# Three products of 256 columns in place of 512 + 256 for the first token half, and weight sums and low parts of the feed-forward stage on GpSimd

## The chip, the cores and the metric

The kernel runs on one core of a Trainium2 chip. The metric is the device time of one execution in microseconds (us), median of several. The core has a matrix engine (TensorE, PE in the profile, its weight loads PEld), three engines for elementwise work (VectorE or DVE, ScalarE or ACT, GpSimd or POOL) and SyncE (SP), whose queue issues the loads here. Matmuls write to PSUM, in banks of 512 float32 columns; weights and activations lie in SBUF.

## The reference, cut to what matters

One layer of an encoder step for two groups of requests that share the weights: 512 prompt tokens and 64 sample tokens, 576 in all, with 1024 features.

```python
xn = _rmsnorm(x, p['ln_mix'])
proj = xn @ p['w_in']
conv_in, z, a, b, qd, kd, vd = jnp.split(proj, SPLIT_AT, axis=-1)
...
oa, S_new = _gdn_chunked(qa, ka, va, g, beta, S0.astype(jnp.float32))
...
ob = _diff_attention(qd.reshape(B, L, H_DIFF, 2, D_DIFF), k_all.reshape(B, Lk, H_DIFF, 2, D_DIFF),
                     v_all, q_pos, k_pos, lam)
...
h = x + jnp.concatenate([oa, ob], axis=-1) @ p['w_out']
h = h + _mem_attn(_rmsnorm(h, p['ln_mem_q']), mem_k, mem_v, p['w_mem_q'], p['w_mem_o'])
hn = _rmsnorm(h, p['ln_ffn'])
h = h + jnp.square(jax.nn.relu(hn @ p['w_ff1'])) @ p['w_ff2']
```

w_ff1 is 1024 x 4096, w_ff2 4096 x 1024; a final norm gives y. Everything is float32.

## The kernel before, in words

**Products in three parts.** Activations are kept transposed, features on the 128 partitions and tokens along the columns. Each operand of a large product is split in two float32r numbers: the high part is a rounding copy (ScalarE), the low part the rest (VectorE, source minus high part). A product is then high x high + high x low + low x high, all summed in one PSUM bank.

**Token halves.** HALVES cuts the 576 tokens into columns 0 to 255 and 256 to 575 (256 and 320 columns). project (line 167) computes one block of 128 output features: for each half it takes a bank "pr" (three of them in turn) and loops over the 128-row slices k of the weights, 8 for a weight of 1024 rows and 4 (kt=4) for a group of the second feed-forward layer. For the second half, high_parts (line 183) issues two matmuls of 320 columns with the high weights, on the tokens' high part and on their low part, and project a third with the low weights. For the first half the two with the high weights are one matmul: its moving operand is both parts side by side, 512 columns, and the bank's two halves take high x high (with low x high added there) and high x low. Every matmul has a weight load of its own.

**The way out of a bank.** project calls evac with the bank and, for the first half, with the bank's other half as "more". add_to (line 191) copies "more" to the target on ScalarE and adds the bank to it on VectorE. The evacs are: conv_input (inputs of the short convolution), project_z, diff_project's evac (q, k, v of the attention heads), add_residual (adds to the residual stream hT, a second time for "more"), split_query, add_group (sums of the second feed-forward layer, likewise a second add) and last_block. The a/b columns (around line 496) go the same way by hand.

**Order of work.** A framework for tiles puts in the semaphores, gives out buffers (a tile waits until the previous owner of its buffer has been read), and sets the order on each engine by priorities (tc.high_priority, tc.issue_after). Each engine then runs its queue in order. First come the norm and the input projection with the convolution; then the chunked scan and the attention heads, with projections between them; the memory keys and values, the output projection, the memory attention; then the feed-forward stage.

**The feed-forward stage** (from about 545 us). The first layer is cut into 16 pairs of 128-column blocks. Each pair (ff1_pair, line 1466) is one step of a two-by-two scheme with seven products instead of eight: split_pair (line 1393) takes the raw quarters A11, A21, A12 and A22 of the pair's weights and forms A21 + A22 (line 1402), A11 - A21 (1407), s1 - A11 (1408) and A12 - A11 (1415), in place but for the first, each 128 x 512 on VectorE; halves_to (lines 1356 and 1357) splits quarters and sums into high (ScalarE) and low parts (VectorE). The products run in the order 1, 5, 6, 2, 7, 3, 4, each 12 matmuls of 288 columns. keep (line 1494) copies an intermediate sum out of a bank on ScalarE, and put applies the squared ReLU and splits the result. The pair's weights lie in tiles "wh", "wl" (two buffers each) and "w4" (three), the raw ones in "raw" (three).

Between pairs run blocks of the second layer, four to a pair: weights2 (line 1462) loads 512 rows of a 128-column block into "r2", split (lines 1455 to 1459) makes "w2h" on ScalarE and "w2l" on VectorE (three buffers each), and project runs with kt=4. split_first forms the first pair's parts on VectorE, and last_weights those of the last group.

Of the kernel before, what the change touches and what calls it, by code (L numbers as in the profile page):

```python
# [15 lines left out]
P = 128  # L16
D = 1024
KT = 8
# [19 lines left out]
def hybrid_layer_kernel(  # L38
# [127 lines left out]

    def project(w, x, evac, kt=KT, halves=HALVES, between=None):


        for a0, n in halves:  # L170
            b = bank("pr")
            for k in range(kt):
                low_part = lambda: mm(b[:, :n], w[1][:, k, :], x[k // 4][:, 0, k % 4, a0 : a0 + n], start=False, stop=False)
                if k == kt - 1:
                    low_part()
                high_parts(b, w[0], x, k, a0, n, kt)
                if k < kt - 1:
                    low_part()
            if between and a0 == 0:
                between()  # L180
            evac(b[:, :n], a0, n, None if a0 else b[:, 256:])

    def high_parts(b, w, x, k, a0, n, kt=KT):
        xk = x[k // 4][:, :, k % 4, a0 : a0 + n]
        if a0 == 0:
            mm(b.rearrange("p (j n) -> p j n", j=2), w[:, k, :], xk, start=k == 0, stop=k == kt - 1)
        else:
            mm(b[:, :n], w[:, k, :], xk[:, 0], start=k == 0, stop=False)
            mm(b[:, :n], w[:, k, :], xk[:, 1], start=False, stop=k == kt - 1)

    def add_to(dst, b, more):
        A.copy(dst, more)
        V.tensor_tensor(dst, b, dst, ALU.add)

# [115 lines left out]
    def conv_input(m, tag="cb"):  # L310
        cbs[m] = cb = small(tag, [P, 584])
        G.memset(cb[:, 0:3], 0.0)

        def evac(b, a0, n, more):
            if a0 == 0 and more is None:
                A.copy(cb[:, 3:259], b)
            elif a0 == 0:
                add_to(cb[:, 3:259], b, more)
            else:
                A.copy(cb[:, 3 + a0 : 259 + a0], b[:, :256])  # L320
                A.copy(cb[:, SOFF + 3 : SOFF + 3 + DEC], b[:, 256:])

        return evac
# [24 lines left out]
    def second(m):  # L348

        a0, n = HALVES[1]  # L350
        b = bank("pr")
        for pw, px in (HH, LH, HL):
            for k in range(KT):
                mm(
                    b[:, :n], wts[m][pw][:, k, :], xs[k // 4][:, px, k % 4, a0 : a0 + n],
                    start=(pw, px) == HH and k == 0, stop=(pw, px) == HL and k == KT - 1,
                )
        ev[m](b[:, :n], a0, n, None)

# [3 lines left out]
    with in_order() as opened:  # L363
# [38 lines left out]
        ev = {4: conv_input(4)}  # L402
        ev[4](fb[4][:, :256], 0, 256, None)
        first(5, HL, LH)
# [11 lines left out]
        ev[5] = conv_input(5)  # L416
        ev[5](fb[5][:, :256], 0, 256, None)
        for q in range(2):
# [3 lines left out]
        ev[6] = conv_input(6, "an")  # L422
        ev[6](fb[6][:, :256], 0, 256, None)
        second(4)
# [71 lines left out]
    for a0, n in HALVES:  # L496
        b = bank("pr")
        for k in range(KT):
            high_parts(b, wab2, xs, k, a0, n)
        if a0:  # L500
            V.tensor_copy(abT[:, a0 : a0 + n], b[:16, :n])
        else:
            add_to(abT[:, :n], b[:16, :256], b[:16, 256:])
    V.tensor_copy(abT[:, T:], abT[:, SEQ:T])
# [132 lines left out]
    def project_z():  # L637
        for h in range(H):
            def evac(b, a0, n, more):
                z = zs[:, h, a0 : a0 + 256]  # L640
                with tc.high_priority():
                    if more is not None:
                        add_to(z, b, more)
                        b = z
                    A.activation(z, b[:, :256], AF.Silu)
                    if a0:
                        A.activation(zsample[:, h, :], b[:, 256:], AF.Silu)

            project(weights(w2, 1536 + h * P), xs, evac)
# [315 lines left out]
    def diff_project(h):  # L965
# [8 lines left out]
        for kind, base in (("q", 2056), ("k", 2568), ("v", 3080)):  # L974
            def evac(b, a0, n, more):
                ts_ = slice(a0, a0 + n)
# [7 lines left out]
                if kind == "q":  # L984
                    d = b
                    if more is not None:
                        d = qn[1][:, ts_].bitcast(F32)
                    with tc.high_priority():
                        if more is not None:
                            add_to(d, b, more)  # L990
                        parts(qn, d)
                    if a0:
                        for c in range(2):
                            R = slice(64 * c, 64 * c + 64)
                            A.copy(qz[R, R], d[R, n - DEC :])
                            for j in range(2):
                                nc.sync.dma_start(
                                    qs[h % 2][64 * j : 64 * j + 64, c, :SEQ].bitcast(F32), qn[j][R].bitcast(F32)
                                )
                    return  # L1000
                d = small("zr", [P, 320])[:, :n] if kind == "v" else kdT[:, h, ts_]
                with tc.high_priority():
                    if more is not None:
                        add_to(d, b, more)
                    else:
                        V.tensor_copy(d, b)
                if kind == "k":
# [206 lines left out]
    def add_residual(m, last, split=None, g0=None, alone=None):  # L1214


        def evac(b, a0, n, more):
            hm = hT[m // 4][:, m % 4, a0 : a0 + n]
            V.tensor_tensor(hm, hm, b, ALU.add)
            if more is not None:  # L1220
                V.tensor_tensor(hm, hm, more, ALU.add)
            if not last:
                return
            if split is not None:
                split_to(split, hm, m, a0, gcol[:, g0 + m : g0 + m + 1])
            if m == 0:
                if a0 == 0:
                    accs[0] = const([P, T], "accq")
                A.activation(accs[0][:, a0 : a0 + n], hm, AF.Square)
            else:  # L1230
                sq = temps(n)
                A.activation(sq, hm, AF.Square)
                if alone is not None:
# [44 lines left out]
    for h in range(H):  # L1278
        qh = [small("kd" if h % 2 else "aT", [P, T], dt=F32R) for i in range(2)]
        ql = cp.tile([P, 2, T], F32R, tag=f"qz{h % 2}", name=nm("ql"))  # L1280
        for i in range(2):
            def split_query(b, a0, n, more):
                if more is not None:
                    q = small("zr", [P, 320])[:, :n]
                    add_to(q, b, more)
                    b = q
                A.copy(qh[i][:, a0 : a0 + n], b)
                V.tensor_tensor(ql[:, i, a0 : a0 + n], b, qh[i][:, a0 : a0 + n].bitcast(F32), ALU.subtract)

            project(weights(w_mem_q[0], (2 * h + i) * P), hx, split_query)  # L1290
# [103 lines left out]
    def split_pair(p):  # L1394
# [6 lines left out]
        with tc.high_priority() if p > 1 else ExitStack():  # L1401
            V.tensor_tensor(s1, A21, b[:, :, P:], ALU.add)
            ws[1] = low_and_high(wtile("wh", wide_))
            halves_to(*ws[1], A11)
            ws[5] = low_and_high(wtile("wh", wide_))
            halves_to(*ws[5], s1)
            V.tensor_tensor(A21, A11, A21, ALU.subtract)
            V.tensor_tensor(A11, s1, A11, ALU.subtract)
            t = [wtile("wl", raw_) for _ in range(2)]
# [4 lines left out]
            ws[2], ws[4] = ([x[:, :, c : c + P] for x in t] for c in (0, P))  # L1414
            V.tensor_tensor(A12, A12, A11, ALU.subtract)
            ws[3] = low_and_high(ft("w4", wide_, 3, F32R))
# [36 lines left out]
    def split(src, tag, bufs, urgent):  # L1453
        shape = list(src.shape)
        wh, wl = (ft(tag + x, shape, bufs, F32R) for x in "hl")
        with tc.high_priority() if urgent else tc.issue_after(put_last[1]):
            A.copy(wh, src)  # L1457
            V.tensor_tensor(wl, src, wh.bitcast(F32), ALU.subtract)  # L1458
        return wh, wl
# [75 lines left out]
    def add_group(g, m):  # L1535
        def evac(b, a0, n, more):
            am = (accu[0] if g < SCALED else hT)[m // 4][:, m % 4, a0 : a0 + n]
            if g == 0:
                if more is not None:
                    add_to(am, b, more)  # L1540
                else:
                    A.copy(am, b)  # L1542
                return
            V.tensor_tensor(am, am, b, ALU.add)  # L1544
            if more is not None:
                V.tensor_tensor(am, am, more, ALU.add)  # L1546

        return evac
# [21 lines left out]
    def last_block(m, s, a0, n, alone=None):  # L1570
        hi, lo = (view(u, m // 4, 16, P)[:, 4 * (m % 4) : 4 * (m % 4) + 4] for u in wlast)

        def evac(b, a0, n, more):
            add_residual(m, True, alone=alone)(b, a0, n, more)
            hm = hT[m // 4][:, m % 4, a0 : a0 + n]
# [141 lines left out]
```

## Time and profile before

| | |
|---|---|
| median of 3 runs | 976.82 us (976.27 to 977.54) |
| span of the profiled execution, first to last instruction | 975.3 us |
| granted TensorE clock, mean | 0.998 |
| feed-forward stage, 550 to 950 us: VectorE busy | 300.95 us |
| the same: ScalarE busy | 215.13 us |
| the same: GpSimd busy | 0.00 us |
| bytes read from memory | 79.93 MB, 92 GB/s over the span with the writes |

The profile is of one execution, and its times are to be compared with its own span; the span leaves out 1.5 us of the median time. In rows of groups stand the line, engine, operation, output and inputs, shapes and count, then the busy time (us) and the mean duration (ns), then idle time before them and who ended it. In rows of the timeline stand start and length in us; matmuls overlap, so their lengths say less than the distance from one start to the next. A release "<-ACT keep L1494" is worked out from semaphores.

### The profile page before, as it was taken

The page shows a single profiled execution, that of the slowest core. Times are in us where ns is not written, and L with a number is a line of the kernel's source. Part 1 is how long each engine was busy: PE and PEld are TensorE (multiplying, and loading weights), DVE is VectorE, ACT ScalarE, POOL GpSimd, SP SyncE. Part 2 cuts the span into 40 slices and gives each one's busy share as a digit, 9 for nine tenths or more (in the row PEclk, how much of TensorE's full clock was granted, in tenths as well). Part 3 has the DMA queues.
Part 4 walks back from the last instruction along what each step waited for, and adds up shares of the span by engine and source line. Part 5 has one row for each costly group of instructions (what it writes and reads, how often), then busy time and mean ns, then how long its engine had stood idle before and what let it go on. Part 6 is the DMA issues. An engine that isn't in the chain of part 4 may idle for free.

```text
span 975.3 us, 16991 instructions
## 1 busy us (share of the span) xinstructions
PE 960.4 (98%) x6399; PEld 889.9 (91%) x6399; DVE 689.4 (71%) x1508; ACT 536.9 (55%) x1218; POOL 66.6 (7%) x158
## 2 busy tenths in 40 slices
PE   9999999998999999999999999999999999999996
PEld 7999998997888878999999999999999999999996
DVE  6655777776867776666657888567867779978674
ACT  6664774533656765435445567665544444545444
POOL 4341020211010000000000000000000000000000
PEclk9999999999999999999999999999999999999999
DMA  7442332120744666341121423332323223322202
GB/s 209 117 138 77 95 125 66 46 64 23 187 122 122 219 182 196 87 130 44 45 65 44 141 69 96 90 88 88 87 81 87 87 87 87 87 87 87 66 23 97
DMA packets 124915, 96.01 MB, mean 98 GB/s; under 512 B 6204, under 2 KB 112846, under 8 KB 124322
## 3 DMA queue, kind: packets, MB, share of 16 engines
q1 hardware_dynamic: 124466, 94.28, 33.6%
q8 instruction: 50, 0.82, 0.4%
q10 hardware_dynamic: 368, 0.66, 0.2%
q14 instruction: 31, 0.25, 0.1%
HBM read 79.93 MB, written 9.75 MB: 92 GB/s over the span
## 4 chain that ended last, share of the span: by engine, by line
PE 58%; issue 2%; DVE 1%; ACT 1%; DMA 0%; POOLq 0%; POOL 0%; ACTq 0%; DVEq 0%; SPq 0%
PE pr L107 37%; PE ba L107 10%; PE g L107 6%; PE gs L107 4%; PE ba L113 1%; DMA raw<-in_w_ff_dram 0%; ACT u L1596 0%; ACT c L1504 0%; DVE u L1552 0%; DVE w2l L1458 0%; ACT c L1503 0%; DVE w L1357 0%; DVE wl L1357 0%; DVE wh L1357 0%; ACT wl L1356 0%
## 5 line engine op out<-in xcount | busy, mean ns | idle before, releaser
L107 PE MATMUL pr<-u,wh 128*128 128x320 f32 (+2 forms) x1240 | 325.9, 341 | 0.1
L107 PE MATMUL pr<-u,wl 128*128 128x256 f32 (+1 forms) x816 | 226.1, 301 | 0.0
L107 PEld LDWEIGHTS pr<-u,wh 128*128 128x128 f32 x1240 | 212.1, 189 | 15.2 <-ACT u L286 0.3
L107 PEld LDWEIGHTS pr<-u,wl 128*128 128x128 f32 x816 | 150.5, 189 | 2.5 <-DVE wl L387 0.2
L160 DVE TENSOR_TENSOR wl<-raw,wh 128x1024 fp32r<-128x1024 f32 x65 | 79.5, 1223 | 56.5 <-ACT wh L159 56.3
L159 ACT CAST wh<-raw 128x1024 fp32r<-128x1024 f32 x65 | 68.2, 1049 | 61.9 <-PE pr L107 46.6
L107 PE MATMUL pr<-u,w2h 128*128 128x320 f32 (+1 forms) x384 | 98.5, 341 | 0.0
L1457 ACT CAST w2h<-r 128x512 fp32r<-128x512 f32 x56 | 34.7, 620 | 87.6 <-PE pr L107 85.4
L107 PE MATMUL pr<-f,w2h 128*128 128x320 f32 (+1 forms) x288 | 74.5, 341 | 0.5 <-DVE u L1546 0.5
L107 PEld LDWEIGHTS pr<-u,w2h 128*128 128x128 f32 x384 | 65.0, 188 | 4.5 <-ACT u L1542 0.3
L107 PE MATMUL pr<-u,w2l 128*128 128x256 f32 (+1 forms) x256 | 65.2, 296 | 0.0
L1544 DVE TENSOR_TENSOR u<-u,pr 128x256 f32<-128x256 f32 x96 | 42.4, 450 | 17.1 <-PE pr L107 16.5
L206 POOL TENSOR_TENSOR tiny<-tiny,nhalf 128x1 f32<-128x1 f32 (+4 forms) x10 | 8.8, 879 | 651.3 <-DVE tiny L1610 514.1
L107 PE MATMUL ba<-u,wl 128*128 128x288 f32 x360 | 52.9, 296 | 0.0
L107 PEld LDWEIGHTS pr<-f,w2h 128*128 128x128 f32 x288 | 48.8, 188 | 4.5 <-issue 1.7
L107 PEld LDWEIGHTS ba<-u,wl 128*128 128x128 f32 x360 | 49.2, 188 | 0.6 <-ACT keep L1494 0.5
L107 PE MATMUL pr<-f,w2l 128*128 128x256 f32 (+1 forms) x192 | 48.9, 295 | 0.0
L107 PEld LDWEIGHTS pr<-u,w2l 128*128 128x128 f32 x256 | 47.0, 189 | 1.5
L1458 DVE TENSOR_TENSOR w2l<-r,w2h 128x512 fp32r<-128x512 f32 x56 | 38.5, 688 | 9.6 <-ACT w2h L1457 9.4
L107 PE MATMUL pr<-wh,u 128*128 128x512 f32 x128 | 41.6, 400 | 0.1
L1503 ACT ACTIVATE c<-c 128x288 f32<-128x288 f32 x48 | 20.6, 443 | 28.5 <-DVE c L1502 28.5
L107 PEld LDWEIGHTS pr<-f,w2l 128*128 128x128 f32 x192 | 35.2, 189 | 1.1
(552 smaller groups left out, 2024.8 us busy)
## 6 DMA issues: line engine op xcount, KB each, us to landing
raw<-in_w_ff_dram SPq DMA_DIRECT2D x36, 512.0 KB
raw<-in_w_in_dram SPq DMA_DIRECT2D x28, 512.0 KB
r<-in_w_ff_dram SPq DMA_DIRECT2D x56, 256.0 KB
raw<-in_w_mem_k_dram SPq DMA_DIRECT2D x8, 512.0 KB
raw<-in_w_mem_v_dram SPq DMA_DIRECT2D x8, 512.0 KB
raw<-in_w_out_dram SPq DMA_DIRECT2D x8, 512.0 KB
raw<-in_w_mem_q_dram SPq DMA_DIRECT2D x8, 512.0 KB
raw<-in_w_mem_o_dram SPq DMA_DIRECT2D x8, 512.0 KB
```

Source lines behind the costliest of these rows:

```text
L107: i = nc.tensor.matmul(out, lhsT, rhs, start=start, stop=stop, skip_group_check=skip_group_check)
L113: i = nc.tensor.transpose(out, in_, ident[:n, :n])
L159: A.copy(wh, raw)
L160: V.tensor_tensor(wl, raw, wh.bitcast(F32), ALU.subtract)
L206: G.tensor_tensor(out, in_, bc(nhalf[: in_.shape[0], 0:1], list(in_.shape)), ALU.pow)
L1457: A.copy(wh, src)
L1458: V.tensor_tensor(wl, src, wh.bitcast(F32), ALU.subtract)
L1503: A.activation(c, c, AF.Relu)
L1544: V.tensor_tensor(am, am, b, ALU.add)
```

## The change

Two things are changed.

First, project runs the three products of both halves alike, as three matmuls of the half's own columns into the same columns of the bank. So evacs get no "more", and add_to and high_parts go; evacs read the bank directly. The a/b columns follow.

Second, in the feed-forward stage the four sums of split_pair and the low part in split (second layer's weights) are issued on GpSimd (G) in place of VectorE (V). halves_to, split_first and last_weights stay as they are.

```diff
-    def project(w, x, evac, kt=KT, halves=HALVES, between=None):
+    def project(w, x, evac, kt=KT, halves=HALVES):
         for a0, n in halves:
             b = bank("pr")
             for k in range(kt):
-                low_part = lambda: mm(b[:, :n], w[1][:, k, :], x[k // 4][:, 0, k % 4, a0 : a0 + n], start=False, stop=False)
-                if k == kt - 1:
-                    low_part()
-                high_parts(b, w[0], x, k, a0, n, kt)
-                if k < kt - 1:
-                    low_part()
-            if between and a0 == 0:
-                between()
-            evac(b[:, :n], a0, n, None if a0 else b[:, 256:])
+                xk = x[k // 4][:, :, k % 4, a0 : a0 + n]
+                passes = [(0, 0), (0, 1), (1, 0)] if k < kt - 1 else [(1, 0), (0, 0), (0, 1)]
+                for j, (jw, jx) in enumerate(passes):
+                    mm(
+                        b[:, :n], w[jw][:, k, :], xk[:, jx],
+                        start=k == 0 and (jw, jx) == (0, 0), stop=k == kt - 1 and j == 2,
+                    )
+            evac(b[:, :n], a0, n)
...
-    def high_parts(b, w, x, k, a0, n, kt=KT):
-        xk = x[k // 4][:, :, k % 4, a0 : a0 + n]
-        if a0 == 0:
-            mm(b.rearrange("p (j n) -> p j n", j=2), w[:, k, :], xk, start=k == 0, stop=k == kt - 1)
-        else:
-            mm(b[:, :n], w[:, k, :], xk[:, 0], start=k == 0, stop=False)
-            mm(b[:, :n], w[:, k, :], xk[:, 1], start=False, stop=k == kt - 1)
-
-    def add_to(dst, b, more):
-        A.copy(dst, more)
-        V.tensor_tensor(dst, b, dst, ALU.add)
...
                 with tc.high_priority():
-                    if more is not None:
-                        add_to(z, b, more)
-                        b = z
                     A.activation(z, b[:, :256], AF.Silu)
...
                 with tc.high_priority():
-                    if more is not None:
-                        add_to(d, b, more)
-                    else:
-                        V.tensor_copy(d, b)
+                    V.tensor_copy(d, b)
...
             V.tensor_tensor(hm, hm, b, ALU.add)
-            if more is not None:
-                V.tensor_tensor(hm, hm, more, ALU.add)
...
         with tc.high_priority() if p > 1 else ExitStack():
-            V.tensor_tensor(s1, A21, b[:, :, P:], ALU.add)
+            G.tensor_tensor(s1, A21, b[:, :, P:], ALU.add)
...
-            V.tensor_tensor(A21, A11, A21, ALU.subtract)
-            V.tensor_tensor(A11, s1, A11, ALU.subtract)
+            G.tensor_tensor(A21, A11, A21, ALU.subtract)
+            G.tensor_tensor(A11, s1, A11, ALU.subtract)
...
-            V.tensor_tensor(A12, A12, A11, ALU.subtract)
+            G.tensor_tensor(A12, A12, A11, ALU.subtract)
...
             A.copy(wh, src)
-            V.tensor_tensor(wl, src, wh.bitcast(F32), ALU.subtract)
+            G.tensor_tensor(wl, src, wh.bitcast(F32), ALU.subtract)
...
             V.tensor_tensor(am, am, b, ALU.add)
-            if more is not None:
-                V.tensor_tensor(am, am, more, ALU.add)
```

conv_input, diff_project's q, split_query and add_group's first group change in the same way as z and k/v: the call of add_to goes, and the copy, cast or difference that followed reads the bank.

More of the change, by code (lines that the diff above doesn't have):

```diff
@@ L312, in conv_input, with evac @@
         G.memset(cb[:, 0:3], 0.0)
-        def evac(b, a0, n, more):
-            if a0 == 0 and more is None:
+        def evac(b, a0, n):
+            if a0 == 0:
                 A.copy(cb[:, 3:259], b)
-            elif a0 == 0:
-                add_to(cb[:, 3:259], b, more)
             else:
@@ L357, in second @@
                 )
-        ev[m](b[:, :n], a0, n, None)
+        ev[m](b[:, :n], a0, n)
     def turn_half(t, q):
@@ L402, in hybrid_layer_kernel @@
         ev = {4: conv_input(4)}
-        ev[4](fb[4][:, :256], 0, 256, None)
+        ev[4](fb[4][:, :256], 0, 256)
         first(5, HL, LH)
@@ L416, in hybrid_layer_kernel @@
         ev[5] = conv_input(5)
-        ev[5](fb[5][:, :256], 0, 256, None)
+        ev[5](fb[5][:, :256], 0, 256)
         for q in range(2):
@@ L422, in hybrid_layer_kernel @@
         ev[6] = conv_input(6, "an")
-        ev[6](fb[6][:, :256], 0, 256, None)
+        ev[6](fb[6][:, :256], 0, 256)
         second(4)
@@ L498, in hybrid_layer_kernel @@
         for k in range(KT):
-            high_parts(b, wab2, xs, k, a0, n)
-        if a0:
-            V.tensor_copy(abT[:, a0 : a0 + n], b[:16, :n])
-        else:
-            add_to(abT[:, :n], b[:16, :256], b[:16, 256:])
+            for j in range(2):
+                mm(b[:, :n], wab2[:, k, :], xs[k // 4][:, j, k % 4, a0 : a0 + n], start=k == j == 0, stop=k == KT - 1 and j == 1)
+        V.tensor_copy(abT[:, a0 : a0 + n], b[:16, :n])
     V.tensor_copy(abT[:, T:], abT[:, SEQ:T])
@@ L638, in project_z, with evac @@
         for h in range(H):
-            def evac(b, a0, n, more):
+            def evac(b, a0, n):
                 z = zs[:, h, a0 : a0 + 256]
                 with tc.high_priority():
-                    if more is not None:
-                        add_to(z, b, more)
-                        b = z
                     A.activation(z, b[:, :256], AF.Silu)
@@ L974, in diff_project, with evac @@
         for kind, base in (("q", 2056), ("k", 2568), ("v", 3080)):
-            def evac(b, a0, n, more):
+            def evac(b, a0, n):
                 ts_ = slice(a0, a0 + n)
@@ L984, in evac @@
                 if kind == "q":
-                    d = b
-                    if more is not None:
-                        d = qn[1][:, ts_].bitcast(F32)
                     with tc.high_priority():
-                        if more is not None:
-                            add_to(d, b, more)
-                        parts(qn, d)
+                        parts(qn, b)
                     if a0:
@@ L994, in evac @@
                             R = slice(64 * c, 64 * c + 64)
-                            A.copy(qz[R, R], d[R, n - DEC :])
+                            A.copy(qz[R, R], b[R, n - DEC :])
                             for j in range(2):
@@ L1002, in evac @@
                 with tc.high_priority():
-                    if more is not None:
-                        add_to(d, b, more)
-                    else:
-                        V.tensor_copy(d, b)
+                    V.tensor_copy(d, b)
                 if kind == "k":
@@ L1214, in add_residual, with evac @@
     def add_residual(m, last, split=None, g0=None, alone=None):
-        def evac(b, a0, n, more):
+        def evac(b, a0, n):
             hm = hT[m // 4][:, m % 4, a0 : a0 + n]
             V.tensor_tensor(hm, hm, b, ALU.add)
-            if more is not None:
-                V.tensor_tensor(hm, hm, more, ALU.add)
             if not last:
@@ L1281, in hybrid_layer_kernel, with split_query @@
         for i in range(2):
[L1282 to L1286, printed above, removed]
+            def split_query(b, a0, n):
                 A.copy(qh[i][:, a0 : a0 + n], b)
@@ L1535, in add_group, with evac @@
     def add_group(g, m):
-        def evac(b, a0, n, more):
+        def evac(b, a0, n):
             am = (accu[0] if g < SCALED else hT)[m // 4][:, m % 4, a0 : a0 + n]
             if g == 0:
[L1539 to L1542, printed above, removed]
+                A.copy(am, b)
                 return
             V.tensor_tensor(am, am, b, ALU.add)
-            if more is not None:
-                V.tensor_tensor(am, am, more, ALU.add)
         return evac
@@ L1571, in last_block, with evac @@
         hi, lo = (view(u, m // 4, 16, P)[:, 4 * (m % 4) : 4 * (m % 4) + 4] for u in wlast)
-        def evac(b, a0, n, more):
-            add_residual(m, True, alone=alone)(b, a0, n, more)
+        def evac(b, a0, n):
+            add_residual(m, True, alone=alone)(b, a0, n)
             hm = hT[m // 4][:, m % 4, a0 : a0 + n]
```

## Prediction

> **What bounds the kernel now.** I read the shares of busy time first, then the chain of work that ended last, then the busy time by stretches.
>
> ```profile
> span 975.3 us, 16991 instructions
> PE 960.4 (98%) x6399; PEld 889.9 (91%) x6399; DVE 689.4 (71%) x1508; ACT 536.9 (55%) x1218; POOL 66.6 (7%) x158
> ...
> PE 58%; issue 2%; DVE 1%; ACT 1%; DMA 0%; POOLq 0%; POOL 0%; ACTq 0%; DVEq 0%; SPq 0%
> ```
> ```profile
> 225.00:350.00 125.00, 121.45 (x784) 105.50 (x783) 90.10 (x284) 77.47 (x250) 9.31 (x22) 1.00 0.51 146
> 550.00:950.00 400.00, 399.18 (x2706) 381.46 (x2705) 300.95 (x579) 215.13 (x455) 0.00 (x0) 1.00 0.29 85
> 950.00:975.30 25.30, 17.43 (x134) 17.17 (x132) 10.25 (x21) 11.14 (x21) 1.55 (x2) 0.91 0.27 93
> ```
>
> TensorE is busy in 98% of the span, and of the chain almost nothing but PE is left. The stretches (columns: length, PE, weight load, DVE, ACT, POOL, each with its count of instructions) say where another engine could matter at all. In the feed-forward stage, 550 to 950 us, PE is idle for 0.8 us of 400, while VectorE has 99 us of its own free and GpSimd does nothing. So a lighter VectorE buys nothing there, and a heavier GpSimd costs nothing until somebody waits for it. Between 225 and 350 us, where the scan and the attention heads run between projections, PE is idle for 3.5 us. The last 25 us hold 7.9 idle us, the output tail, which the change doesn't enter. "Busy" hides how fast matmuls follow each other, so the question is the distance from one start to the next.
>
> **Part 1: one matmul of 512 columns becomes two of 256.** Today a step k of the first token half is 512 + 256 columns (high weights on both parts, low weights on the high part); afterwards it is three times 256. The products are the same, the columns too. What differs is one more matmul, and one more weight load, per step. The count of steps is the count of 512-column groups into bank pr:
>
> ```profile
> L107 PE MATMUL pr<-u,wh 128*128 128x512 f32 x392 | 145.6, 401 | 0.0
> ...
> L107 PE MATMUL pr<-u,w2h 128*128 128x512 f32 x128 | 48.3, 398 | 0.0
> ...
> L107 PE MATMUL pr<-f,w2h 128*128 128x512 f32 x96 | 36.2, 398 | 0.0
> ...
> L107 PE MATMUL pr<-f,u 128*128 128x512 f32 x32 | 10.8, 398 | 0.0
> ...
> L107 PE MATMUL pr<-u,wab 128*128 128x512 f32 x8 | 2.0, 392 | 0.0
> ```
>
> 392 + 128 + 96 + 32 + 8 = 656 steps. (The x128 of pr<-wh,u are the memory keys and values, which the diff leaves alone.) For the pace I take stretches of the timeline in which nothing waits. The durations of 0.28 and 0.40 us overlap, so only the starts in the first column count:
>
> ```profile
> 34.95 0.39 PE L107 MATMUL pr<-u,wh 128*128 128x512 f32 x1
> 35.18 0.28 PE L107 MATMUL pr<-u,wl 128*128 128x256 f32 x1
> ...
> 37.07 0.40 PE L107 MATMUL pr<-u,wh 128*128 128x512 f32 x1
> ```
> ```profile
> 400.09 0.40 PE L107 MATMUL pr<-u,wh 128*128 128x512 f32 x1
> ...
> 401.86 0.40 PE L107 MATMUL pr<-u,wh 128*128 128x512 f32 x1
> ```
> ```profile
> 447.14 0.28 PE L107 MATMUL gs<-u,aT 128*128 128x256 f32 x1
> ...
> 449.15 0.39 PE L107 MATMUL pr<-u,wh 128*128 128x512 f32 x1
> ...
> 449.85 0.39 PE L107 MATMUL pr<-u,wh 128*128 128x512 f32 x1
> ```
> ```profile
> 702.95 0.40 PE L107 MATMUL pr<-u,w2h 128*128 128x512 f32 x1
> ...
> 703.64 0.40 PE L107 MATMUL pr<-u,w2h 128*128 128x512 f32 x1
> ```
>
> Pairs of 512 + 256: six in 37.07 - 34.95 = 2.12 us, five in 401.86 - 400.09 = 1.77, two in 449.85 - 449.15 = 0.70, two in 703.64 - 702.95 = 0.69. That is 15 pairs in 5.28 us, 0.3520 us each. From 447.14 to 449.15 stand 17 matmuls of 256 columns, each with weights of its own: 2.01 / 17 = 0.1182 us, so three take 0.3547. A step grows by 2.7 ns, and 656 steps by **1.8 us**. For bounds: the two longest rows (11 pairs in 3.89 us, 0.3536) give 1.1 ns and 0.7 us; the feed-forward pair alone (0.345) gives 9.7 ns for its 256 steps, 2.5 us, and with 1.1 ns for the other 400 about 2.9 us. Rounding of starts at 10 ns moves either by about 1 us, so I keep **0 to 4 us**. All of it is on the path, since PE bounds nearly every stage.
>
> **Part 2: the sums of two half banks go.** Before, the low product lies in the other half of the bank, and add_to (a copy on ScalarE, then an add on VectorE) or a second add brings it over.
>
> ```profile
> L1546 DVE TENSOR_TENSOR u<-u,pr 128x256 f32<-128x256 f32 x48 | 20.0, 417 | 0.7
> ...
> L1221 DVE TENSOR_TENSOR u<-u,pr 128x256 f32<-128x256 f32 x24 | 10.1, 419 | 0.4
> ...
> L193 DVE TENSOR_TENSOR u<-pr,u 128x256 f32<-128x256 f32 x18 | 7.4, 413 | 1.7 <-ACT u L192 1.4
> ...
> L192 ACT COPY u<-pr 128x256 f32<-128x256 f32 x18 | 6.7, 371 | 7.8 <-PE pr L107 7.8
> ```
>
> Removed are 72 second adds (30.1 us of VectorE) and, by the code, 42 calls of add_to (9 convolution inputs, the a/b columns, 4 z, 12 attention projections, 8 memory queries, 8 blocks of the first group). Each frees up to 0.37 us of ScalarE and 0.41 us of VectorE; several keep one plain copy. In the feed-forward stage this lies beside a PE that is never idle: worth nothing. Where PE does wait, in the 3.5 us between 225 and 350, the same evacuations (4 z, 12 attention projections) get shorter by about 0.8 us each, off the scan's own chain. I count -0.4 us for the middle, with 0 and -3.5 us (all of that idle time) as ends. New evacuations wait for the same last matmul of a bank, and no buffer is held longer.
>
> **Part 3: GpSimd takes 60 sums of quarters and 56 low parts.** VectorE's prices now, and the nearest GpSimd rows:
>
> ```profile
> L1458 DVE TENSOR_TENSOR w2l<-r,w2h 128x512 fp32r<-128x512 f32 x56 | 38.5, 688 | 9.6 <-ACT w2h L1457 9.4
> ...
> L1402 DVE TENSOR_TENSOR s<-raw,raw 128x512 f32<-128x512 f32 x15 | 10.4, 693 | 6.6 <-DMA raw<-in_w_ff_dram 6.3
> ```
> ```profile
> L806 POOL TENSOR_TENSOR tg<-tg,tg 128x4 f32<-128x4 f32 x4 | 0.8, 200 | 35.9 <-DVE tg L805 35.9
> ...
> L483 POOL TENSOR_TENSOR triu<-triu,ones 128x128 f32<-128x128 f32 x1 | 0.5, 460 | 0.0
> ```
>
> From 4 to 128 columns GpSimd grows by (460 - 200) / 124 = 2.1 ns a column, so 512 columns take 200 + 508 x 2.1 = 1.27 us, an estimate. Its ends are 0.69 (as on VectorE) and 4 x 0.46 = 1.84 us (no fixed part). I take 1.27: 116 of them are 147 us in 400. The Trainium skill, "GPSIMD Engine Reference", section 3.1, has the same add 1.96 times slower than on VectorE; by that, 1.35 us, an estimate of the page's. VectorE loses 60 x 0.69 + 56 x 0.69 = 80 us, and with the second adds about 105 of its 301.
>
> What must not come late is a weight. One pair of the first layer, beside its neighbours (rows in order of time: start, length, engine):
>
> ```profile
> 694.39 0.69 DVE L1357 TENSOR_TENSOR wh<-raw,wh 128x512 fp32r<-128x512 f32 x1
> ...
> 695.39 0.69 DVE L1408 TENSOR_TENSOR raw<-s,raw 128x512 f32<-128x512 f32 x1
> ...
> 699.85 1.04 ACT L1356 CAST wl<-raw 128x1024 fp32r<-128x1024 f32 x1
> ...
> 700.80 0.39 ACT L1494 COPY keep<-ba 128x288 f32<-128x288 f32 x1
> ...
> 701.24 1.63 PEld L107 LDWEIGHTS ba<-u,w 128*128 128x128 f32 x12 [0.27 <-ACT keep L1494]
> ...
> 704.35 0.69 DVE L1415 TENSOR_TENSOR raw<-raw,raw 128x512 f32<-128x512 f32 x1
> ...
> 705.19 0.61 ACT L1356 CAST w<-raw 128x512 fp32r<-128x512 f32 x1
> ```
>
> The third sum (L1408) must follow the low part at 694.39, which reads the quarter that it overwrites. On GpSimd it would end near 695.1 + 1.3 = 696.4, against 696.08 now; the cast that reads it starts only at 699.85, when PE gives up the buffer: 3.4 us to spare. The fourth (L1415) would end at 705.6 and hold back the cast of 705.19 by 0.5 us; that weight is used in the next pair, behind four blocks of some 3 us. Behind that cast on ScalarE stand only parts of the pair's outputs, due as late. The second layer's low part comes 0.6 us later after its cast; the cast begins when the block three back is through, so two blocks lie ahead, 6 us against 0.62 + 1.27. Its raw buffer is then freed 0.6 us later, so SP's queue, which waits there in order, issues the next loads 0.6 us later, into the same 6 us. No DMA moves to GpSimd's queue, and its queue holds nothing else in this stage. Cost on the path: **0**, as long as that cover holds.
>
> Sum: 1.8 - 0.4 + 0 = 1.4 us on the profiled span of 975.3; on the median of 976.8, which holds 1.5 us more than the span, **978.2 us**. A difference of 0.2% (2 us) is about what a measurement of this kernel can tell from no change.
>
> **The rivals.**
> - *GpSimd's sums hold ScalarE up (slower).* The place is the cast at 699.85: ScalarE works in order, keep stands right behind it, and PE waits for keep already (0.27 us in the row of 701.24). It decides from the point at which the third sum comes more than 3.4 us late. Two things could do that: a queue on GpSimd in which sum and low parts stand in a bad order, and VectorE and GpSimd getting in each other's way, which this trace can't show, since GpSimd never works there. A delay of 0.3 to 0.9 us in each of 15 pairs adds 4.5 to 13 us; with 0.6 us, 9 us, **987 us**. Against it: the 3.4 us, and a GpSimd that is 147 / 400 = 37% full. The Trainium skill, "SBUF — State Buffer", section "Who interferes with whom", speaks against the change here: a VectorE instruction with two SBUF inputs and a GpSimd one that reads SBUF lock each other out for a whole instruction. By that rule all of GpSimd's 147 us can fall on VectorE; from the rows, 301 - 105 + 147 = 343 us of 400, still under PE, so the rule by itself costs nothing until the ops come to (400 - 196) / 116 = 1.76 us. Chance 0.22.
> - *The lighter evacuations help the middle (faster).* If the projections' shorter ways out let scan and heads run earlier, PE gets back most of its 3.5 idle us between 225 and 350, and some idle time drawn as busy: -5 + 1.8, **973.6 us**. For it: VectorE is 72% busy there. Against it: the idle time sits in dependent chains that contain none of the removed sums. Chance 0.19.
> - *The two halves don't overlap as said.* If the second weight load (0.19 us) weren't hidden, 656 x (0.19 - 0.12) = 46 us, **1023 us**. The 17 matmuls at 447.14 each load weights and keep 0.118 us. Chance 0.02.
>
> **How the numbers follow.** Forecast 0.57, 976.4 to 980.4 (part 1 from 0 to 4, the middle's 0.4 off); of that 0.35 within 0.2% and 0.22 slower. The GpSimd rival 0.22 slower, the middle rival 0.13 faster and 0.06 within, the weight load 0.02 slower. Together: faster 0.13, same 0.41, slower 0.46. The range from 973.5 to 987 leaves out some 0.2: half of the faster rival's far side, the upper half of GpSimd's, the weight load.
>
> **What would show it.** PE counts 7055 matmuls, and starts of 256 columns stand 0.118 us apart through a first half. GpSimd shows 116 tensor-tensors of about 1.27 us between 550 and 950, VectorE about 196 us there, and PE's idle time there stays near 0.8 us. I am wrong if PE waits for casts or keep, if 256-column steps pace over 0.120 us, or if the stretch from 225 to 350 us changes by more than its idle time.

## The result, and the profile after

The changed kernel takes **982.52 us** (median of 4 runs, 982.17 to 984.60), the kernel before, on the same chip, 977.18 us (4 runs): a ratio of **1.0058**, 95% interval 1.0046 to 1.0070. By the ratio it is slower by 5.7 us, where 1.4 had been forecast. The execution that was profiled took 982.87 us, with a span of 981.1.

The page of the changed kernel, its totals:

```profile
span 981.1 us, 18157 instructions
...
PE 964.8 (98%) x7055; PEld 926.1 (94%) x7055; DVE 625.3 (64%) x1287; ACT 527.7 (54%) x1191; POOL 227.5 (23%) x274
```

TensorE still fills 98% of the span, now with 7055 matmuls (6399 + 656). VectorE is lighter by 64 us and GpSimd heavier by 161, and neither of these two numbers says where the 5.7 us come from. The stretches do (length, PE, weight load, DVE, ACT, POOL, each with its count; then granted clock, DMA share, GB/s):

```profile
225.00:350.00 125.00, 123.62 (x850) 111.00 (x849) 86.58 (x269) 75.08 (x243) 9.73 (x20) 1.00 0.53 149
...
535.00:650.00 115.00, 111.19 (x825) 109.80 (x824) 71.24 (x108) 71.71 (x148) 39.55 (x29) 1.00 0.34 99
...
550.00:950.00 400.00, 395.63 (x2946) 391.07 (x2945) 245.54 (x388) 213.79 (x449) 161.06 (x116) 1.00 0.28 83
```

Against the rows of before in the prediction: between 225 and 350 us PE's idle time has fallen from 3.55 to 1.38 us, and in the feed-forward stage, 550 to 950, it has risen from 0.82 to 4.37. All but a little of the latter lies before 650 us (115.00 - 111.19 = 3.81). There PE waits as the list of waits says (who waits, for what, the idle us in all, how often, the longest); before, then after:

```profile
PEld ba L107 <- ACT keep L1494: 2.5, 10, 0.3
```
```profile
PEld ba L107 <- ACT keep L1460: 7.8, 16, 2.3
```
```profile
PE ba L107 <- ACT keep L1460: 3.9, 4, 2.0
```

L1460 is L1494 of before: the copy `keep` on ScalarE. The wait that the prediction named as the place of its first rival has grown. The timeline of the changed kernel shows it twice, in the first pairs (start, length, engine; in brackets the idle time before and what ended it):

```profile
586.36 0.62 ACT L1423 CAST w2h<-r 128x512 fp32r<-128x512 f32 x1 [1.04 <-DMA r<-in_w_ff_dram]
...
587.75 0.38 ACT L1460 COPY keep<-ba 128x288 f32<-128x288 f32 x1
...
588.18 1.87 PE L107 MATMUL ba<-u,wl 128*128 128x288 f32 x12 [1.17 <-ACT keep L1460]
...
603.02 1.29 POOL L1368 TENSOR_TENSOR s<-raw,raw 128x512 f32<-128x512 f32 x1 [3.69 <-DMA raw<-in_w_ff_dram]
...
604.39 1.29 POOL L1373 TENSOR_TENSOR raw<-raw 128x512 f32<-128x512 f32 x1
...
605.77 1.61 POOL L1374 TENSOR_TENSOR raw<-s,raw 128x512 f32<-128x512 f32 x1
...
607.41 1.04 ACT L1322 CAST wl<-raw 128x1024 fp32r<-128x1024 f32 x1 [0.33 <-POOL raw L1374]
...
608.71 0.38 ACT L1460 COPY keep<-ba 128x288 f32<-128x288 f32 x1
...
609.14 1.87 PE L107 MATMUL ba<-u,w 128*128 128x288 f32 x12 [2.05 <-ACT keep L1460]
```

From 603 us on, read one chain downwards: the first three sums on GpSimd, one behind the other without a gap, the cast of the third on ScalarE, and only then `keep`, because ScalarE works in order. PE has stood still for 2.05 us by then. These are the weights of pair 3 (pairs are counted from 0), made while pair 2 runs. At 586 another cast, of the second layer's weights, stands ahead of `keep` and waits for a load, and PE loses 1.17 us. The load isn't later than elsewhere: where the first low parts are left on VectorE, in the third experiment below, the same cast starts only at 588.87, also behind its load, but there `keep` (587.55) stands ahead of it in ScalarE's queue, and that wait is gone.

The other half of the loss is the pace, which no share of busy time shows. The timeline of the changed kernel in a first half (only the starts count):

```profile
553.24 0.28 PE L107 MATMUL pr<-u,wl 128*128 128x256 f32 x1
...
555.04 0.28 PE L107 MATMUL pr<-u,wl 128*128 128x256 f32 x1
```

Five steps in 1.80 us, 0.360 us each and so 0.120 us for each matmul of 256 columns, against 0.3520 us for a step before. Of the 2192 distances from the start of a matmul of 256 columns to the next start in this trace 1519 are 120 ns exactly. This row gives 8 ns a step. Over both whole traces, waits left out, the mean distance behind a matmul of 256 columns into `pr` is 119.6 ns in the changed kernel, 358.7 for three; before, it is 234.7 behind 512 columns and 117.9 behind 256, 352.6 for a step. That is **6 ns a step, 4.0 us for the 656**, if none of it is hidden.

### The profile page after: what moved, and what is told of

It is laid out like the page before. It is cut to its first block, busy times and chain, and to the rows that moved or that the text cites. A ratio compares the mean times of both kernels' runs of the same rounds, so it can differ in the third digit from the quotient of the medians.

```text
span 981.1 us, 18157 instructions
## 1 busy us (share of the span) xinstructions
PE 964.8 (98%) x7055; PEld 926.1 (94%) x7055; DVE 625.3 (64%) x1287; ACT 527.7 (54%) x1191; POOL 227.5 (23%) x274
## 4 chain that ended last, share of the span: by engine, by line
PE 89%; ACT 3%; issue 2%; DMA 2%; DVE 1%; POOL 1%; SPq 0%; POOLq 0%; ACTq 0%; DVEq 0%
PE pr L107 56%; PE g L107 11%; PE ba L107 11%; PE gs L107 7%; PE ba L113 3%; PE g L113 2%; DMA u<-in_mem_prompt_dram 1%; DMA raw<-in_w_in_dram 1%; DMA r<-in_w_ff_dram 0%; DVE p L444 0%; DMA raw<-in_w_ff_dram 0%; ACT wh L159 0%; PE gs L113 0%; DVE w L1323 0%; ACT p L1030 0%
## 5 line engine op out<-in xcount | busy, mean ns | idle before, releaser
L107 PE MATMUL pr<-u,wh 128*128 128x256 f32 (+1 forms) x1632 | 333.2, 300 | 0.2
L107 PEld LDWEIGHTS pr<-u,wh 128*128 128x128 f32 x1632 | 258.8, 190 | 1.5 <-DVE u L278 0.3
L107 PEld LDWEIGHTS pr<-u,wl 128*128 128x128 f32 x816 | 147.9, 190 | 0.7 <-DVE wl L372 0.2
L1424 POOL TENSOR_TENSOR w2l<-r,w2h 128x512 fp32r<-128x512 f32 x56 | 79.6, 1429 | 63.5 <-ACT w2h L1423 63.4
L107 PEld LDWEIGHTS pr<-u,w2h 128*128 128x128 f32 x512 | 79.6, 190 | 0.9 <-issue 0.6
L107 PE MATMUL pr<-f,w2h 128*128 128x256 f32 (+1 forms) x384 | 73.1, 296 | 0.0
L107 PEld LDWEIGHTS pr<-f,w2h 128*128 128x128 f32 x384 | 59.6, 190 | 0.0
L1368 POOL TENSOR_TENSOR s<-raw,raw 128x512 f32<-128x512 f32 x15 | 20.5, 1367 | 134.5 <-DMA raw<-in_w_ff_dram 134.5
L1381 POOL TENSOR_TENSOR raw<-raw,raw 128x512 f32<-128x512 f32 x15 | 20.2, 1348 | 117.6 <-DVE w L1323 117.6
L107 PEld LDWEIGHTS pr<-u,w2l 128*128 128x128 f32 x256 | 44.9, 190 | 0.0
```

The source lines that it names most:

```text
L107: i = nc.tensor.matmul(out, lhsT, rhs, start=start, stop=stop, skip_group_check=skip_group_check)
L1368: G.tensor_tensor(s1, A21, b[:, :, P:], ALU.add)
L1381: G.tensor_tensor(A12, A12, A11, ALU.subtract)
L1424: G.tensor_tensor(wl, src, wh.bitcast(F32), ALU.subtract)
```

## The experiments

**The theory after the result**: part 1 costs what the pace of 0.120 us says, less what the lighter evacuations save between 225 and 350 us; the other 4 us are GpSimd's. The rivals: part 1 alone makes the whole loss, or GpSimd costs nothing but its first pairs, or it costs something all through by keeping VectorE from its operands. All kernels compute the whole reference. "Ratio" is always to the kernel before on the same chip, with its 95% interval.

**Each part alone.** In the first kernel sums and low part are back on VectorE (five lines), so that it holds parts 1 and 2 of the prediction; the second is the kernel before with those five lines on GpSimd.

```
-            G.tensor_tensor(s1, A21, b[:, :, P:], ALU.add)
+            V.tensor_tensor(s1, A21, b[:, :, P:], ALU.add)
...
-            G.tensor_tensor(wl, src, wh.bitcast(F32), ALU.subtract)
+            V.tensor_tensor(wl, src, wh.bitcast(F32), ALU.subtract)
```

> The changed kernel with the four sums and the low part back on VectorE: only the three products of 256 columns are left of the change. Theory (three terms: every first-half step is 7 ns longer, 656 steps, +4.6 us; GpSimd makes the first pairs of the feed-forward stage wait, +3.9 us; the lighter evacuations give the middle back 3 us): ratio to before 1.0016 (+1.6 us), PE's waits for keep back from 3.9 + 7.8 to about 2.5 us, starts of 256-column matmuls 0.120 us apart. Rival 1 (the whole loss is the pace and GpSimd only moves idle time about): ratio 1.005 to 1.006, as the full change. Rival 2 (the pace costs what was predicted, 1.8 us, and GpSimd all the rest): below before, ratio 0.998 to 0.999.

Measured: 979.22 us (11 runs; before 977.60), ratio **1.0017** (1.0008 to 1.0026). The split alone costs 1.7 us of the 5.7; the other 4.0 us (0.0041 of 977) are what GpSimd adds to it. The sum fits: 4.0 us of pace less some 2 us that PE idles less between 225 and 350 us.

> The kernel before with the four sums and the second layer's low part on GpSimd: only the second part of the change. Theory: +3.9 us, ratio 1.004, with PE's new idle time between 580 and 615 us and almost none later. Rival 1 (GpSimd costs nothing by itself, only beside the denser PE): ratio 1.000. Rival 2 (VectorE and GpSimd lock each other out all through the stage): +5 to +13 us, ratio 1.005 to 1.013, spread over all pairs.

Measured: 998.85 us, ratio **1.0220** (1.0206 to 1.0234). Neither theory nor rivals had that: +21.5 us, five times what GpSimd costs in the full change. A row of its list of waits:

```profile
PE pr L107 <- DVE u L1546: 10.7, 5, 2.2
```

The wait for `keep` is there too. This one is new: PE waits 2.2 us, five times, for the add on VectorE that frees a `pr` bank. The timeline of this kernel at one of the five:

```profile
809.58 1.93 DVE L1506 TENSOR_TENSOR c<-c,rB 128x288 f32<-128x288 f32 x2
...
809.80 1.38 POOL L1415 TENSOR_TENSOR raw<-raw,raw 128x512 f32<-128x512 f32 x1 [8.41 <-DVE w L1357]
...
812.77 1.52 POOL L1458 TENSOR_TENSOR w2l<-r,w2h 128x512 fp32r<-128x512 f32 x1 [1.58 <-ACT w2h L1457]
...
813.10 1.51 DVE L1509 TENSOR_TENSOR f<-c,f 128x288 fp32r<-128x288 f32 x1
...
814.53 0.41 DVE L1546 TENSOR_TENSOR u<-u,pr 128x256 f32<-128x256 f32 x1
...
815.09 0.53 PE L107 MATMUL pr<-u,w2h 128*128 128x320 f32 x2 [2.16 <-DVE u L1546]
```

The difference on VectorE, 288 columns, takes 1.51 us while GpSimd's low part runs beside it, where others of its size take 0.45, and ends 0.3 us after it. Some 3.5 us earlier the same has happened beside the fourth sum: two products on VectorE take 1.93 us together, where two in a row elsewhere take 0.82. Behind both stands the add, and behind the add PE; two delays of about 1.1 us are the 2.2 us that PE waits. That is VectorE and GpSimd getting in each other's way, the second half of the prediction's first rival, at another place.

**Which of GpSimd's instructions.** First, VectorE keeps the sums of the pairs 1 and 2 and the low parts of the first three blocks (`urgent` is false there):

```
-            G.tensor_tensor(s1, A21, b[:, :, P:], ALU.add)
+            (G if p > 2 else V).tensor_tensor(s1, A21, b[:, :, P:], ALU.add)
...
-            G.tensor_tensor(wl, src, wh.bitcast(F32), ALU.subtract)
+            (G if urgent else V).tensor_tensor(wl, src, wh.bitcast(F32), ALU.subtract)
```

> The changed kernel, but the sums of pairs 1 and 2 and the first three blocks' low parts stay on VectorE; from pair 3 on GpSimd does them as in the change. Theory (only the pairs without second-layer blocks between them have no cover): nearly all of GpSimd's 3.9 us goes, ratio to before 1.002 (+1.6 to +2.5 us), PE's waits for keep near 3 us. Rival (the cost is spread over all pairs, or comes from the lock): at most a fifth of it goes, ratio 1.005.

Measured: 983.64 us, ratio 1.0053 (1.0039 to 1.0067). The theory's 1.002 missed; the rival's number came. Yet the trace shows a reason other than the rival's: the chain above belongs to pair 3, which was still on GpSimd (timeline of this kernel):

```profile
602.50 1.64 POOL L1368 TENSOR_TENSOR s<-raw,raw 128x512 f32<-128x512 f32 x1 [164.31 <-DVE w2l L1424]
...
605.59 1.60 POOL L1374 TENSOR_TENSOR raw<-s,raw 128x512 f32<-128x512 f32 x1
...
607.22 1.04 ACT L1322 CAST wl<-raw 128x1024 fp32r<-128x1024 f32 x1 [0.32 <-POOL raw L1374]
...
608.95 3.17 PE L107 MATMUL ba<-u,w 128*128 128x288 f32 x12 [2.45 <-ACT keep L1460]
```

From the first sum's start to the cast of the third sum are 4.72 us. In the kernel of the split alone, with the same three sums on VectorE (and other work between them), they are 3.13 us, and `keep` stands ahead of the cast in ScalarE's queue:

```profile
602.12 0.69 DVE L1368 TENSOR_TENSOR s<-raw,raw 128x512 f32<-128x512 f32 x1
...
604.47 0.40 ACT L1460 COPY keep<-ba 128x288 f32<-128x288 f32 x1 [1.00 <-PE ba L107]
...
605.25 1.05 ACT L1322 CAST wl<-raw 128x1024 fp32r<-128x1024 f32 x1 [0.39 <-DVE raw L1374]
```

So two things differ, the length of the chain and the order of the queue, which is set anew when a kernel is built; no run separates them. Either way one more pair on VectorE should end the cost (`p > 3` in place of `p > 2`):

> The changed kernel with the sums of pairs 1, 2 and 3 and the first three blocks' low parts on VectorE, GpSimd from pair 4 on: one pair more on VectorE than in e5_early_on_v, whose trace still had PE wait 2.5 us for keep while ScalarE stood before a sum of pair 3. Theory: that wait goes, and the half-speed clock behind it; ratio to before 1.0015 to 1.0025, PE's waits for keep near 3 us. Rival (the wait moves on to the next pair that GpSimd gets): ratio 1.005 as in e5_early_on_v.

Measured: 979.45 us (11 runs), ratio **1.0019** (1.0010 to 1.0027), against 1.0017 for the split alone. GpSimd at work from pair 4 on, 101 instructions of the 116, costs nothing that can be measured. Its stretch from 600 to 615 us shows a PE that never waits, beside the next kernel's, where it waits for 2.45 us:

```profile
600.00:615.00 15.00, 15.00 (x116) 15.00 (x116) 11.95 (x19) 10.68 (x25) 2.33 (x2) 1.00 0.63 186
```

**Sums or low parts.** The changed kernel with the low part on VectorE (only the sums on GpSimd), then with the sums on VectorE (only the low parts on GpSimd), by the same lines as above.

> The changed kernel with the second layer's low part back on VectorE: three products of 256 columns, and of the GpSimd work only the four sums of each pair. Theory (the slower chain sum, cast, low part, sum, cast makes ScalarE's copy keep late in pairs 1 to 3): most of GpSimd's cost stays, ratio to before 1.004 to 1.006, PE waiting about 2 us for keep near 607 us. Rival (the low parts on GpSimd hold up the sums or the loads): near the split alone, ratio 1.0015 to 1.0025.

Measured: 984.59 us, ratio 1.0073 (1.0060 to 1.0085), above the theory's 1.004 to 1.006. The wait for `keep` near 607 us is there as said, in its stretch PE is idle for 2.45:

```profile
600.00:615.00 15.00, 12.55 (x94) 12.33 (x95) 10.19 (x15) 8.77 (x21) 5.99 (x4) 1.00 0.43 123
```

> The changed kernel with the four sums back on VectorE: three products of 256 columns, and of the GpSimd work only the second layer's low part. Theory (low parts have two blocks of cover): as the split alone, ratio to before 1.0015 to 1.0025, PE's waits for keep near 2.5 us. Rival (locks against VectorE through the stage): ratio 1.004 or more.

Measured: 986.40 us, ratio **1.0096** (1.0083 to 1.0110). The theory's 1.0015 to 1.0025 fell, the rival's 1.004 and more came. Its list of waits has the row of the second kernel again, and the timeline the same picture:

```profile
PE pr L107 <- DVE u L1507: 5.2, 5, 1.1
```
```profile
809.06 1.91 DVE L1475 TENSOR_TENSOR f<-c,f 128x288 fp32r<-128x288 f32 x2
809.12 1.54 POOL L1424 TENSOR_TENSOR w2l<-r,w2h 128x512 fp32r<-128x512 f32 x1 [13.23 <-ACT w2h L1423]
...
810.89 1.14 DVE L1507 TENSOR_TENSOR u<-u,pr 128x256 f32<-128x256 f32 x3
...
811.35 0.56 PE L107 MATMUL pr<-u,w2h 128*128 128x320 f32 x2 [1.04 <-DVE u L1507]
```

The parts don't add up: over the split alone, sums alone cost 0.0056 (5.5 us), low parts alone 0.0079 (7.7 us), both together 0.0041 (4.0 us). In the changed kernel at the same place the add comes at 809.99 us and the low part starts only at 812.00, so the add isn't behind it, and the waits of 1.1 us aren't there. In the second kernel, which also has the second adds on VectorE, the fourth sum and the low part both hold an instruction ahead of the add, and the wait is 2.2 us; what sets which instruction stands where hasn't been tested. PE's idle time between 550 and 950 us goes the same way:

| kernel | PE idle, 550 to 950 us | ratio |
|---|---|---|
| before | 0.8 | 1 |
| split alone | 0.6 | 1.0017 |
| GpSimd from pair 4 on | 0.5 | 1.0019 |
| both parts (the change) | 4.4 | 1.0058 |
| sums alone on GpSimd, split | 4.3 | 1.0073 |
| low parts alone on GpSimd, split | 7.2 | 1.0096 |
| both on GpSimd, no split | 15.9 | 1.0220 |

The sums alone lose some 1.7 us more against the split alone than these idle times say. Most of that isn't in the profiled executions, whose spans are 981.9 and 977.6 us, 4.3 apart, with 3.8 of it idle: this kernel's times go from 982.96 to 985.51 us, and the profiled one took 984.01.

**Where the split pays and where it costs.** The kernel before with three products of 256 columns in z and the attention projections only (16 first halves, 128 of the 656 steps), then in all the others only (528 steps):

```
+    def project(w, x, evac, kt=KT, halves=HALVES, between=None, apart=False):
...
+            if apart:
+                for k in range(kt):
...
+                    for j, (jw, jx) in enumerate(passes):
+                        mm(b[:, :n], w[jw][:, k, :], xk[:, jx], ...)
+                evac(b[:, :n], a0, n, None)
```

> The kernel before, with three products of 256 columns only in the 4 projections of z and the 12 of the attention heads (128 of the 656 steps); all else, the feed-forward stage too, as before. Theory (the middle gains because these evacuations get shorter): -3 us + 128 x 7 ns = -2.1 us, ratio 0.998, the stretch from 125 to 350 us shorter by about 2 us. Rival (the middle's gain comes from other projections or from a chance order of the work): ratio 1.000 to 1.002.

Measured: 976.58 us (11 runs; before 977.60), ratio **0.9990** (0.9981 to 0.9999), its interval just under 1. It is the only kernel here that is faster than the kernel before, by 0.1%. Its stretch, beside 121.45 us of PE before:

```profile
225.00:350.00 125.00, 123.63 (x849) 111.10 (x848) 86.08 (x268) 75.97 (x244) 10.47 (x20) 1.00 0.53 150
```

PE works 2.2 us more in these 125, and 128 steps at 6 ns cost 0.8 us: a gain of 1.4, and 1.0 was measured.

> The kernel before with three products of 256 columns everywhere except in the projections of z and of the attention heads (528 of the 656 steps): the complement of e6_split_middle, all sums on VectorE. Theory (a step costs 7 ns more, and the gain lies in the middle): +528 x 7 ns = +3.7 us, ratio 1.0035 to 1.004. Rival 1 (a step costs 2.7 ns as predicted): +1.4 us, ratio 1.0015. Rival 2 (the gain comes from the evacuations everywhere): ratio 1.000 to 1.001.

Measured: 980.11 us, ratio **1.0029** (1.0018 to 1.0040), somewhat under the 1.0035 expected. In its stretch from 225 to 350 us PE is busy for 121.41 us, as before: nothing is gained without the middle. 2.9 us over 528 steps are 5.4 ns each, and the interval allows 3.3 to 7.4: the 6 ns of the starts lie in it, the 2.7 of the prediction don't. Both kernels together, -1.0 + 2.9 = 1.9 us, are the split alone (1.7).

**What a matmul costs by its columns.** The changed kernel with the first half of `w_out` cut into 128 + 128, 192 + 64 or 256 columns, by block; of it only starts are read, in stretches in which nothing waits.

```
+        project(..., add_residual(m, True, hx, G_Q), cut=((128, 128), (192, 64), None)[m % 3])
```

> The changed kernel, but in the output projection (8 blocks, a stretch in which PE waits for nothing) the first half is cut further: blocks 0, 3, 6 into 128 + 128 columns, blocks 1, 4, 7 into 192 + 64, blocks 2 and 5 stay at 256. Only the starts of the matmuls are read. Theory (a matmul with its own weights costs (columns + 32) / 2.4 ns, the 32 a fixed price): starts 66.7 ns apart at 128 columns, 93.3 at 192, 40.0 at 64, 120.0 at 256, 146.7 at 320. Rival (the weight load sets a floor): no less than about 108 ns for any of them, as transposes of 128 columns show; 2.7 ns of fixed price, as the prediction had it: 56, 83 and 30 ns.

From its timeline:

```profile
380.94 0.27 PE L107 MATMUL pr<-u,wl 128*128 128x128 f32 x1
...
385.97 0.28 PE L107 MATMUL pr<-u,wl 128*128 128x128 f32 x1
...
386.43 0.31 PE L107 MATMUL pr<-u,wl 128*128 128x320 f32 x1
...
388.63 0.31 PE L107 MATMUL pr<-u,wl 128*128 128x320 f32 x1
...
389.86 0.27 PE L107 MATMUL pr<-u,wl 128*128 128x192 f32 x1
...
391.87 0.27 PE L107 MATMUL pr<-u,wl 128*128 128x192 f32 x1
```

45 matmuls of 128 columns in 5.03 us and 18 of 192 in 2.01 us go at 0.112 us each, 15 of 320 in 2.20 us at 0.147; 256 columns keep 0.120. From 256 to 320 columns 64 more take 27 ns, 2.4 columns a ns, and the theory, columns + 32 at that rate, gives both distances (0.120 and 0.147); below, a floor as the rival had it, at some 0.111 us, is what counts. What sets the floor isn't shown.

## Why the prediction was right and wrong

The direction, slower, and the range, 973.5 to 987, held; the forecast of 978.2 us was 4.3 us too low, and by its own bounds of 976.4 to 980.4 the likeliest case was the wrong one. None of the three terms had its size: one was 2 us too small, one 4 us, and one erred by 2 us the other way, so that the range held is the rivals' doing and in part luck.

**Part 1, +1.8 us, was mis-sized.** The prediction took 0.1182 us for a matmul of 256 columns from the one stretch of before in which such matmuls follow each other, in the memory attention. In the projections of the changed kernel the same size goes at 0.1196 in the mean. Multiplied by three and 656 the missing 1.4 ns are 2.7 us; a step of before that is 0.6 ns longer than the 0.3520 of the prediction's rows takes 0.4 back. A step grows by 6 ns by the starts (4.0 us) and by 5.4 ns (3.6 us) by the runs of the 528 steps, so the term was half its size or less, and the bounds of 0 to 4 us just held it. Nothing in before would have given 0.1196: there matmuls of 256 columns are followed after 0.118 us in the projections too. Why they go slower in the changed kernel stays open.

**Part 2, -0.4 us, had the right place and too small a size.** PE got back 2.2 of its 3.55 idle us between 225 and 350, in the changed kernel and with the middle split alone (1.5 to 2.2 in the other kernels that split there); where the middle was left out, nothing. The bound of 3.5 held. The argument that the idle chains contain none of the removed sums was wrong in effect: VectorE and ScalarE are 72 and 62% full there, and what they are spared may let others come forward; which chain got shorter hasn't been traced. This was the second rival, at half its price.

**Part 3, 0, is the step that failed**, at the words "as long as that cover holds". The reserve of 3.4 us was read from one pair near 700 us, and in the pairs like it it holds: from pair 4 on GpSimd costs nothing beside the split. The first pairs have no such reserve. No blocks of the second layer stand between them yet, the sums start as late as their loads arrive, and there the three sums in a row take 4.7 us in place of 3.1 up to the cast (GpSimd from pair 3 in the third experiment, VectorE in the first). The prediction had put one sum behind its low part, and not three behind each other. It also took ScalarE's queue as given, where the order of casts and `keep` changed with the engines. So the first rival happened, at its place, cast ahead of `keep`, with a price of 4.0 us and not 9: in the first pairs and not in each. Only the wait of 2.05 us hangs on a sum; the 1.17 us hang on a load. The wait of 0.27 us that the prediction read as PE's, in the row of 701.24, is one of the weight load; in the kernel before PE's own list has no wait for `keep`.

**The price of one instruction** was near: 1.27 us said, and by the groups of the changed kernel:

```profile
L1424 POOL TENSOR_TENSOR w2l<-r,w2h 128x512 fp32r<-128x512 f32 x56 | 79.6, 1429 | 63.5 <-ACT w2h L1423 63.4
...
L1368 POOL TENSOR_TENSOR s<-raw,raw 128x512 f32<-128x512 f32 x15 | 20.5, 1367 | 134.5 <-DMA raw<-in_w_ff_dram 134.5
```

Undisturbed, as at 603.02 above, it is 1.29 us. VectorE's load was not near: 196 us said between 550 and 950, 245.5 measured. Beside the split alone (278.31 us there), 80 us of work left and its busy time fell by only 33. The missing 47 us are instructions that got longer. The groups show which; the changed kernel, then the split alone (count, busy us, mean ns):

```profile
L1475 DVE TENSOR_TENSOR u<-c,u 128x288 fp32r<-128x288 f32 x32 | 20.4, 661 | 10.6 <-ACT u L1474 10.5
L1507 DVE TENSOR_TENSOR u<-u,pr 128x256 f32<-128x256 f32 x48 | 19.8, 412 | 13.1 <-PE pr L107 13.1
...
L1323 DVE TENSOR_TENSOR wh<-s,wh 128x512 fp32r<-128x512 f32 x15 | 16.6, 1106 | 12.9 <-ACT wh L1322 12.9
```
```profile
L1507 DVE TENSOR_TENSOR u<-u,pr 128x256 f32<-128x256 f32 x48 | 19.9, 415 | 3.4 <-PE pr L107 2.5
...
L1475 DVE TENSOR_TENSOR u<-c,u 128x288 fp32r<-128x288 f32 x32 | 14.1, 452 | 7.4 <-ACT u L1474 7.4
...
L1323 DVE TENSOR_TENSOR wh<-s,wh 128x512 fp32r<-128x512 f32 x15 | 10.4, 690 | 2.3 <-ACT wh L1322 2.3
```

With two operands in SBUF the mean grows from 452 to 661 ns and from 690 to 1106; the add that reads a bank of PSUM stays (415 and 412). The Trainium skill, "SBUF — State Buffer", section "Who interferes with whom", has exactly this division, and the traces agree with it. The prediction's use of that rule, that it costs nothing while VectorE is below full, was right for the change from pair 4 on and is wrong in general: with the low parts alone on GpSimd VectorE is 64% busy (255.96 us of 400 by its stretch), and PE waits for single adds all the same.

**The third rival**, a weight load that isn't hidden, was rightly set at little: PE's steps grew by 6 ns and not by 70. The counts (7055 matmuls, 116 instructions on GpSimd) came as said; of the three conditions for being wrong, the wait for `keep` was met.

## What to carry to other kernels

A reserve read from one iteration holds for iterations like it: look at the first ones by themselves, where the work that gives the cover hasn't begun. The pace of a matmul can differ by a ns or two from one kernel to another, which counts when it is multiplied by thousands: the kernel before had 256 columns at 0.118 us in the mean, in the projections as in the memory attention, so a short trial of the new order was the only way to its pace. Work moved to GpSimd is cheap only where nothing in order behind the VectorE instruction beside it frees a buffer that TensorE is waiting for; here that meant leaving the sums of pairs 1 to 3 on VectorE, and splitting only where the saved evacuations shorten a stage in which TensorE waits (the two together weren't run).

## What the runs showed of the hardware

**A fixed share per matmul.** Each with its own weights, matmuls of 256 and 320 columns start 0.120 and 0.147 us apart, which is 0.107 and 0.133 us for the columns at the 2.4 a ns worked out above and some 13 ns on top; at 192 and 128 columns the distance stays at 0.111 to 0.112 us, which by the same sum is what 235 columns would cost. In the kernel before, 256 columns take 0.118. The Trainium skill, "TensorE: Matmul & The Clock Gate", section "Wait — 56ns, not 53.3ns?", has 2.5 ns on top; for these matmuls the measurement decides.

**A short wait can lower the clock.** After the wait of 2.45 us in the kernel that keeps pairs 1 and 2 on VectorE, the granted clock fell (its stretches; the clock is the third number from the end):

```profile
604.00:608.30 4.30, 2.49 (x19) 2.27 (x18) 1.61 (x3) 2.14 (x4) 3.03 (x3) 1.00 0.61 172
608.30:611.00 2.70, 2.05 (x9) 2.05 (x10) 2.33 (x4) 2.58 (x6) 0.00 (x0) 0.64 0.00 0
```

12 matmuls behind that wait took 3.17 us. Not every such wait does it: with the sums alone on GpSimd PE waits just as long at the same place, and the clock stays at 1.00 (timeline and stretch of that kernel):

```profile
608.47 1.87 PE L107 MATMUL ba<-u,w 128*128 128x288 f32 x12 [2.45 <-ACT keep L1460]
```
```profile
608.30:611.00 2.70, 2.54 (x20) 2.54 (x20) 2.55 (x5) 2.58 (x7) 0.00 (x0) 1.00 0.00 0
```

Nor did the wait of 2.05 us in the changed kernel, while one of 1.96 us in the second kernel, near 607 us, was followed by 12 matmuls in 2.85 us. So the length of the wait alone doesn't decide, and what does isn't shown. What it costs is: of the five executions of the kernel with pairs 1 and 2 on VectorE three had a mean clock of 0.996 and took 983.64 to 983.99 us, two had 0.998 and took 980.75 and 981.30. That accounts for how its median, with less idle time than the change, came out no faster. In the second kernel the waits of 2.2 us go with a mean clock of 0.75 to 0.87 in the 6 us around each of the three that were read, and its 15 us of idle time with a loss of 21.5.
